# A two-layer hybrid diffusion trunk on one core: reordered modulation and attention, quarter products and a moved copy in the recurrent mixer

## The chip, the cores and the metric

The kernel runs on one core of one Trainium2 chip. The time is device microseconds of one execution; several executions of the same program are summarised by their median. The engines are PE (TensorE, matmuls; PEld is its weight load), DVE (VectorE), ACT (ScalarE), POOL (GpSimd) and SP (SyncE, which here only issues DMAs). ACT and POOL issue DMAs as well.

## The reference

Two layers are applied to 640 tokens: 128 prompt (context) tokens and 512 latent tokens, D = 1024. Cut to what matters:

```python
def trunk_layer(x, mod, P, l, ctx_cache):
    shift1, scale1, gate1, shift2, scale2, gate2 = jnp.split(mod, 6, axis=-1)   # mod = silu(c) @ w_mod[l] + b_mod[l]
    h = rms_norm(x, P['norm_mix_pre'][l]) * (1.0 + scale1) + shift1
    o, cache = mixer(h, P, l, ctx_cache)      # z = h @ w_in; heads of A, B and C; o = concat @ w_out
    x = x + gate1 * rms_norm(o, P['norm_mix_post'][l])
    h = rms_norm(x, P['norm_ffn_pre'][l]) * (1.0 + scale2) + shift2
    gu = h @ P['w_gu'][l]
    f = (jax.nn.silu(gu[..., :FF_DIM]) * gu[..., FF_DIM:]) @ P['w_down'][l]
    return x + gate2 * rms_norm(f, P['norm_ffn_post'][l]), cache

def wkv_step(S, inp):                          # mixer C: 6 heads of 64, two directions
    r, w, k, v, a, b = inp
    sa = jnp.einsum('bhvk,bhk->bhv', S, a)
    S = S * w[:, :, None, :] + sa[..., None] * b[:, :, None, :] + v[..., None] * k[:, :, None, :]
    return S, jnp.einsum('bhvk,bhk->bhv', S, r)
```

Mixers A (4 heads, window and sink) and B (6 heads, normed q and k) are softmax attention. The prompt has its own conditioning vector.

## The kernel before, in words

One program of `trunk_kernel` (L211) runs both layers. Tokens stand in five tiles of 128, taken in the order 4, 1, 2, 0, 3 (tile 4 is the prompt). Large weights are split into a high and a low part (`split`, a cast on ACT at L364 and a subtraction on DVE at L365), and each such product is three matmuls. A layer has these stages, in order:

- **Modulation.** `mod_pieces` (L466) makes a list of pieces from `mod_bias` (L415 to L419), `mod_chunk` (L384 to L391) and `mod_rows` (L421 to L450). A chunk loads 512 KB of `w_mod` as 128 rows of four pieces of 256 numbers, and multiplies it with four matmuls into four groups of 32 columns of one PSUM bank (L391). A group (one third of a layer's modulation) has 16 chunks. Group (0, 0) runs at the start of the program through `raw_tile`, a ring of three slots, beside the loads of x, which ACT issues (L562). Groups (0, 1) and (0, 2) run inside the attention loop of layer 0, two pieces at every second step. Layer 1's groups take another way (`mod_part`, DVE) during the FFN of layer 0.
- **Norm and in-projection.** `norm_tile` (L505) squares (L509), scales (L511, L512), transposes on PE (L517) and applies the modulation (L521, L524), then splits (L528, L529). `mm_tile` (L613 to L620) makes the heads; its weights come through SP (L377).
- **Attention.** A `Unit` (L791) is one pair of query heads by query tile: scores (L812, L813), peak (L829 to L844), norm (L846), turn (transposes, L853 to L865), mix (L867 to L874). The loop at L892 runs scores of unit n, then norm and turn of unit n − LAG, then mix of unit n − LAG − LAG2, with LAG = LAG2 = 1. A scheduler sets the order of the instructions on each engine there.
- **Recurrent mixer.** Five groups g of 128 tokens. `front(g)` (L1039 to L1142) prepares decays (tanh L1051, L1063), keys and gates (L1068 to L1088), and, per direction d and half cc of the group, the products of b and k with W (L1100): six matmuls into two PSUM tiles, one per head of a pair, with two copies by ACT (L1105) and two masks by DVE (L1106) and two more masks into W (L1109). `front` ends in 24 small matmuls (L1119) whose result goes to memory as `dN` (L1122). `relay(g)` (L1144 to L1159) reads it back, inverts the 16x16 blocks with 30 small POOL instructions (L1152, L1154), makes a transposed copy `VT` with DVE (L1156) and writes both to `dV`, `dW` (L1158). `solve(g)` loads them (L1166) and multiplies (L1174, L1185, L1195); `rec`, `bonus` and `finalize` follow. PE's order is written by hand: a string `WEAVE` names the stream that gives PE's next piece, under `tc.manual_schedule(engines={PE})` (L1446).
- **Out-projection, FFN.** `mm_fm` (L537) and `mm_tm` (L547).

PE, DVE, ACT and POOL each take their instructions in order, so an instruction that waits holds what is behind it on its engine. SP's DMAs are issued in order too.

Of the kernel before, what the change touches and what calls it, by code (L numbers as in the profile page):

```python
# [13 lines left out]
AF = mybir.ActivationFunctionType  # L14
# [7 lines left out]
KD = 8  # L22
# [16 lines left out]
WEAVE = ("aqqaaqaqaqqaqqqaaqqaqaqqqaqaaqqqqqqqqqccababbbbbccccbbcddcbdbcdcbbdcbdbgdcbddgeggegegeggffggegefgfgeeeeeehfgffgjjjjjjhffjihhhhjhjhhhjjhjjhjmmijikiiiimiimmkkmmmlkkmmmmkmkklklkllkklrlnnllnnmvonmnvnnrnrnvnonoovvvoorwwpooropprwwwsspwsssswpspswswppppwuppwttwtxstwuuyttxttyuuyxtutututttuutuuuuu",  # L39
         "aqqaaqaqaqqaqqqaaqqaqaqqqaqaaqqqqqqqqqccababbbbbccccbbcddcbdbcdcbbdcbdbgdcbddgeggegegeggffggegefgfgeeeeeehfgffgjjjjjjhffjihhhhjhjhhhjjhjjhjmmijikiiiimiimmkkmmmlkkmmmmkmkklklkllkklrlnnllnnmvonmnvnnrnrnvnonoovvvoorwwpooropprwwwsspwsssswpspswswppppwuppwttwtxstwuuyttxttyuuyxtutututttuutuuuuu")  # L40
# [82 lines left out]
def places(mem):  # L123
# [39 lines left out]
    mem.lay("N", 0, ("VD", 768), ("WD", 768), ("U", 256), ("tp", 64))  # L163
    mem.lay("M", 0, *many("W", (0, 1), 1536), *many("GB", (0, 1), 768), *many("TK", (2, 3), 768), *many("E", (0, 1), 384), *many("Xi", (0, 1), 384))
# [46 lines left out]
def trunk_kernel(ctx, tc, I, O, dbg=None, depth=DEPTH):  # L211
# [254 lines left out]
    def mod_pieces(groups, ps, n, slot, dma, ac=None, ahead=2):  # L466

        pieces = []
        for l, gi in groups:
            pieces.append(lambda l=l, gi=gi: mod_bias(ps, l, gi, slot()[0:4, 0:512]))  # L470
# [5 lines left out]
            else:  # L476
                for k in range(KD):
                    for c0 in range(0, 512, n):
                        pieces.append(lambda l=l, gi=gi, k=k, c0=c0: mod_chunk(ps, l, gi, k, c0, n, slot()[:, 0:4 * n], dma))
            pieces.append(lambda l=l, gi=gi: mod_rows(l, gi, ps, slot()[:, 0:512]))  # L480
        live = deque()
        for f in pieces + [None] * ahead:
            if f is not None:
                live.append(f())
                next(live[-1])
            if f is None or len(live) > ahead:
                next(live.popleft(), None)
                yield
# [16 lines left out]
    def norm_tile(p_, xt, hg, sc, sh):  # L505
        xn, h32 = nt["xn"](), nt["h32"]()
        tk = slice(128 * p_, 128 * p_ + 128)
        ssq = small.tile([128, 1], F32, tag="nss", name="nss")
        nc.scalar.activation(out=xn, in_=xt, func=AF.Square, accum_out=ssq)  # L509
# [45 lines left out]
    for l in range(depth):  # L555
        if True:
            acc = bank(0, 1, 4, 5, 6)
            if l == 0:
                hg = open_h()
                open_nt(2)  # L560
                for t in ORDER:
                    nc.scalar.dma_start(out=xt[t], in_=I["x_sample"][0, 128 * t:128 * t + 128] if t < 4 else I["x_prompt"][0])  # L562
                run(mod_pieces([(0, 0)], psb[:, 7], 256, raw_tile, nc.sync))
# [20 lines left out]

            cs = mem.get("cs", [4, 2, 32])
# [1030 lines left out]
```

## Time and profile before

| what | before |
|---|---|
| median of 3 runs | 2181.96 us (2177.76 to 2182.04) |
| the profiled execution | 2174.8 us |
| its span | 2172.8 us |
| mean granted TensorE clock | 0.953 |
| PE busy | 1972.3 us (91%) |
| PEld busy | 1727.2 us (79%) |
| DVE busy | 1205.6 us (55%) |
| ACT busy | 829.4 us (38%) |
| POOL busy | 348.6 us (16%) |
| DMA | 192.13 MB, mean 88 GB/s |

Times in the rows are microseconds from the start of the span, unless a mean is given in ns. A busy share is an average over stages with different limits; so the stretches of the program are read one by one below. A row such as "7.29 <-DVE F L1051" says that the engine stood idle for 7.29 us and that the DVE instruction of line 1051 ended it. The granted clock is the share of full speed that the throttle gave to TensorE: 0.50 is 1.2 GHz, 1.00 is 2.4 GHz.

### The profile page before, as it was taken

To read this page: it belongs to the slowest core of one execution; us is meant where nothing else is said; L and a number is where in the kernel's file an instruction comes from. 1 tells how busy PE (TensorE), PEld (TensorE's weight loads), DVE (VectorE), ACT (ScalarE), POOL (GpSimd) and SP (SyncE) were. 2 spreads that over 40 slices of the span, in tenths; PEclk is the share of its full clock that TensorE was granted. 3 is DMA by queue.
4 is the path that set the end of the run, shared out by engine and by line. 5 is a ranking of instruction groups with operands and counts; after the bars stand their busy time and mean duration, and the time that the engine had idled before them with its cause. 6 is when DMAs were issued, how large, how long until landed. Compare 5 with 4: busy or idle time off the path is not lost. (4 is left out here: it accounts for less than half of the span.)

```text
span 2172.8 us, 39707 instructions
## 1 busy us (share of the span) xinstructions
PE 1972.3 (91%) x16220; PEld 1727.2 (79%) x16220; DVE 1205.6 (55%) x2369; ACT 829.4 (38%) x1827; POOL 348.6 (16%) x634
## 2 busy tenths in 40 slices
PE   4989998777999999999989999877789999999997
PEld 1766787666779989989977778866677898998996
DVE  1756754565877636566367784356667622232324
ACT  2545643342463222212245674433335522221221
POOL 0210003353022112111022000234421100000002
PEclk8999998888999999999999999977899999999998
DMA  8265211213336344344222002031242222222221
GB/s 275 82 192 163 73 36 30 37 31 69 103 116 181 122 141 146 118 145 121 82 96 80 9 1 69 14 50 26 52 127 83 88 78 78 78 66 81 78 69 49
DMA packets 280765, 192.13 MB, mean 88 GB/s; under 512 B 107316, under 2 KB 249614, under 8 KB 280584
## 3 DMA queue, kind: packets, MB, share of 16 engines
q1 hardware_dynamic: 259152, 139.41, 23.2%
q0 software_dynamic: 8800, 29.17, 4.4%
q10 hardware_dynamic: 12632, 21.03, 2.9%
q8 instruction: 127, 2.08, 0.4%
q14 instruction: 54, 0.44, 0.1%
HBM read 173.48 MB, written 16.08 MB: 87 GB/s over the span
## 5 line engine op out<-in xcount | busy, mean ns | idle before, releaser
L537 PE MATMUL psb<-H,B 128*128 128x320 f32 x2112 | 318.3, 311 | 3.1 <-DVE H L529 2.4
L537 PEld LDWEIGHTS psb<-H,B 128*128 128x128 f32 x2112 | 312.3, 189 | 7.7 <-DVE H L529 3.2
L537 PE MATMUL psb<-H,A 128*128 128x320 f32 x2016 | 306.0, 311 | 0.0
L537 PEld LDWEIGHTS psb<-H,A 128*128 128x128 f32 x2016 | 298.4, 189 | 2.2 <-issue 1.2
L365 DVE TENSOR_TENSOR A<-F,A 128x1024 fp32r<-128x1024 f32 (+1 forms) x78 | 93.3, 1196 | 137.9 <-ACT A L364 137.9
L365 DVE TENSOR_TENSOR B<-F,B 128x1024 fp32r<-128x1024 f32 (+1 forms) x78 | 94.1, 1208 | 131.4 <-ACT B L364 131.4
L494 POOL TENSOR_TENSOR r<-v,F 128x1 f32<-128x1 f32 (+1 forms) x50 | 41.9, 840 | 739.4 <-DVE v L492 728.5
L364 ACT CAST B<-F 128x1024 fp32r<-128x1024 f32 x80 | 83.0, 1037 | 179.9 <-PE psb L537 112.8
L364 ACT CAST A<-F 128x1024 fp32r<-128x1024 f32 (+1 forms) x78 | 80.0, 1025 | 187.1 <-PE psb L537 94.3
L537 PE MATMUL psb<-H,C 128*128 128x320 f32 x864 | 130.6, 309 | 0.0
L537 PEld LDWEIGHTS psb<-H,C 128*128 128x128 f32 x864 | 127.8, 188 | 0.2
L405 DVE SCALAR_TENSOR_TENSOR F<-F 128x512 f32<-128x512 f32 x168 | 114.7, 748 | 19.9 <-DMA F<-in_w_mod 14.4
L397 POOL DMA_DIRECT2D F<-in_w_mod x96 | 71.9, 749 | 327.1 <-DVE F L403 216.9
L1544 DVE TENSOR_TENSOR F<-F,psb 128x320 f32<-128x320 f32 x88 | 42.9, 487 | 121.9 <-PE psb L537 121.9
L547 PE MATMUL psb<-A,M 128*128 128x512 f32 x370 | 96.7, 390 | 0.0
L365 DVE TENSOR_TENSOR C<-F,C 128x1024 fp32r<-128x1024 f32 (+1 forms) x34 | 40.5, 1193 | 78.2 <-ACT C L364 78.1
L547 PEld LDWEIGHTS psb<-A,M 128*128 128x128 f32 x370 | 69.2, 188 | 15.4 <-issue 1.0
L831 DVE TENSOR_REDUCE mx<-psb 128x1 f32<-128x640 f32 (+3 forms) x100 | 64.4, 645 | 30.2 <-PE psb L813 25.8
L547 PE MATMUL psb<-B,M 128*128 128x512 f32 x310 | 77.6, 390 | 0.0
L1538 ACT ACTIVATE F<-psb 128x320 f32<-128x320 f32 x88 | 38.3, 435 | 97.1 <-PE psb L537 96.0
L364 ACT CAST C<-F 128x1024 fp32r<-128x1024 f32 (+1 forms) x34 | 34.7, 1022 | 91.8 <-PE psb L547 46.6
L547 PEld LDWEIGHTS psb<-B,M 128*128 128x128 f32 x310 | 58.0, 188 | 12.8 <-issue 0.8
(418 smaller groups left out, 3960.3 us busy)
## 6 DMA issues: line engine op xcount, KB each, us to landing
F<-in_w_gu SPq DMA_DIRECT2D x88, 512.0 KB
F<-in_w_mod POOLq DMA_DIRECT2D x96, 256.0 KB, 3.4
F<-in_w_in SPq DMA_DIRECT2D x40, 512.0 KB
F<-in_w_down SPq DMA_DIRECT2D x40, 512.0 KB
F<-in_w_mod SPq DMA_DIRECT2D x38, 512.0 KB
M<-in_w_mod SPq DMA_DIRECT2D x10, 512.0 KB
F<-in_w_out SPq DMA_DIRECT2D x40, 128.0 KB
F<-in_x_sample ACTq DMA_DIRECT2D x8, 512.0 KB
```

Of the source, the lines that this page charges most:

```text
L364: nc.scalar.copy(out=hi[:, :n], in_=rawt[:, :n])
L365: (eng or nc.vector).tensor_tensor(out=lo[:, :n], in0=rawt[:, :n], in1=hi[:, :n], op=ALU.subtract)
L397: dma.dma_start(out=rv, in_=w[:, :, c0:c0 + n])
L405: nc.vector.scalar_tensor_tensor(out=ac[s][:, cc], in0=r[:, cc], scalar=sT[:, k, s:s + 1], in1=ac[s][:, cc], op0=ALU.mult, op1=ALU.add)
L494: nc.gpsimd.tensor_tensor(out=r, in0=v, in1=mhalf.to_broadcast(shape), op=ALU.pow)
L537: nc.tensor.matmul(out=ps2[hf][:, :HALF], lhsT=w[:, k, :], rhs=a[k][:, tk], start=(k == 0 and q == 0), stop=(k == KD - 1 and q == 2))
L547: nc.tensor.matmul(out=ps5[t], lhsT=a[k][:, tk], rhs=w[:, kk, :], start=(first and kk == 0 and q == 0), stop=(last and kk == nk - 1 and q ...
L831: nc.vector.reduce_max(out=mx, in_=self.S, axis=AX.XY if self.nb == 5 else AX.X)
L1538: nc.scalar.activation(out=sgt[:, HALF * hf:HALF * hf + HALF], in_=pg[hf][:, :HALF], func=AF.Silu)
L1544: nc.vector.tensor_tensor(out=sgt[:, tk], in0=sgt[:, tk], in1=pu[hf][:, :HALF], op=ALU.mult)
```

## The change

Five edits. (1) A modulation chunk is two DMAs of 128 x 1024 contiguous numbers and four matmuls of 512 columns, instead of one DMA of 128 x 4 x 256 and, over two chunks, eight matmuls of 256 columns. At the start the ring has 18 slots of 512 KB, and nine chunks are under way at once; x is scaled before the modulation is there (`scale_tile`), and the loads of tables and caches move from ACT's queue to SP's, behind `w_mod`. (2) In layer 0's attention the ring is three pairs of slots, two chunks are issued ahead of the loop and one at every second step. (3) LAG is 2, and PE's order in the attention loops is written out. (4) In `front` the products of b and k are 64 x 64 quarters: twelve matmuls for six, ordered so that one PSUM tile gets what ACT copies and DVE masks at once. (5) `VT` is copied by POOL. The WEAVE strings are new. Lines of the changed kernel are higher by 2 to 29.

```diff
-KEYS, AHEAD, LAG, LAG2, VALS, PRE = 10,2,1,1,2,'kqf'
+KEYS, AHEAD, LAG, LAG2, VALS, PRE = 10, 2, 2, 1, 2, 'kqf'
-MODW, BES = 512, 1
+MODW, BES, XA = 512, 1, 5
...
-    def mod_chunk(ps, l, gi, k, c0, n, r, dma):
...
-        dma.dma_start(out=rv, in_=w[:, :, c0:c0 + n])
+    def mod_chunk(ps, l, gi, k, r2, dma):
+
+        rv = [r.rearrange("p (j c) -> p j c", j=2) for r in r2]
+        for h in range(2):
+            o = 2048 * gi + 1024 * h
+            dma.dma_start(out=r2[h], in_=I["w_mod"][l, 128 * k:128 * k + 128, o:o + 1024])
         yield
         for j in range(4):
-            nc.tensor.matmul(out=ps[32 * j:32 * j + 32, c0:c0 + n], lhsT=sT[:, k, :], rhs=rv[:, j], start=False, stop=(k == KD - 1 and c0 + n == 512))
+            nc.tensor.matmul(out=ps[32 * j:32 * j + 32, :], lhsT=sT[:, k, :], rhs=rv[j // 2][:, j % 2], start=False, stop=k == KD - 1)
...
+                load_x(nc.scalar, ORDER[:XA])
+
+                mp = [mem.get(f"mp{i}", [1024]) for i in range(18)]
+                mg0 = mod_pieces([(0, 0)], psb[:, 7], 512, Ring([mp[i:i + 2] for i in range(0, 18, 2)]), nc.sync, None, 9)
+                run(mg0, 9)
+                load_x(nc.sync, ORDER[XA:])
+                for t in ORDER:
+                    scale_tile(xt[t])
+                run(mg0)
...
-                    norm_tile(t, xt[t], hg, (l, "sc1", s), (l, "sh1", s))
+                    norm_tile(t, xt[t], hg, (l, "sc1", s), (l, "sh1", s), px, True)
...
+            ceng = nc.sync if l == 0 else nc.scalar
...
-                    nc.scalar.dma_start(out=head2(dst[:, 0])[:, :, y], in_=I[nm][0, l])
+                    ceng.dma_start(out=head2(dst[:, 0])[:, :, y], in_=I[nm][0, l])
...
-                mslot = Ring([mem.get(nm, [1024]) for nm in ("mv0", "mv1", "mw2")])
-                mg = mod_pieces([(0, 1), (0, 2)], psb[:, 7], 256, mslot, nc.sync)
+                close_w("raw")
+                ms = [mem.get(nm, [1024]) for nm in ("raw0", "raw1", "raw2", "mw2", "mv0", "mv1")]
+                mg = mod_pieces([(0, 1), (0, 2)], psb[:, 7], 512, Ring([ms[i:i + 2] for i in range(0, 6, 2)]), nc.sync)
+                run(mg, 2)
...
-            for n_ in range(len(units) + 4):
-                if n_ % 2 == 0:
-                    run(mg, 2)
+            with tc.manual_schedule(engines={PE}):
+                for n_ in range(len(units) + 5):
+                    if n_ % 2 == 0:
+                        run(mg, 1)
...
-                        pv2 = [v3(pf(), w=128) for e in range(2)]
+                        pb, pk = v3(pf(), w=128), v3(pf(), w=128)
                         for pr in range(3):
                             for e in range(2):
-                                nc.tensor.matmul(out=pv2[e][:, pr], lhsT=BK[HS[e], pr, cc, e:e + 2].rearrange("p a j -> p (a j)"), rhs=W[HS[e], e, pr, cc],
-                                                 start=True, stop=True)
+                                for h, pv in ((e, pb), (1 - e, pk)):
+                                    nc.tensor.matmul(out=pv[HS[h], pr], lhsT=BK[HS[e], pr, cc, int(h != e)], rhs=W[HS[e], e, pr, cc], start=True, stop=True)
+
+                        nc.scalar.copy(out=GB[:, cc, :, 0:64], in_=pb[:, :, 0:64])
+                        nc.vector.tensor_tensor(out=GB[:, cc, :, 64:128], in0=pb[:, :, 64:128],
+                                                in1=mK[d][:, 64:128].unsqueeze(1).to_broadcast([128, 3, 64]), op=ALU.mult)
                         for e in range(2):
-                            pv = pv2[e]
-
-                            nc.scalar.copy(out=GB[HS[e], cc, :, 0:64], in_=pv[HS[e], :, 0:64])
-                            nc.vector.tensor_tensor(out=GB[HS[e], cc, :, 64:128], in0=pv[HS[e], :, 64:128],
-                                                    in1=mK[d][HS[e], 64:128].unsqueeze(1).to_broadcast([64, 3, 64]), op=ALU.mult)
                             o = HS[1 - e]
-                            nc.vector.tensor_tensor(out=W[o, e, :, cc], in0=pv[o], in1=mK[d][o].unsqueeze(1).to_broadcast([64, 3, 128]), op=ALU.mult)
-                            yield
+                            nc.vector.tensor_tensor(out=W[o, e, :, cc], in0=pk[o], in1=mK[d][o].unsqueeze(1).to_broadcast([64, 3, 128]), op=ALU.mult)
+                        yield
...
-                nc.vector.tensor_copy(out=VT, in_=V.rearrange("p s t -> p t s"))
+                nc.gpsimd.tensor_copy(out=VT, in_=V.rearrange("p s t -> p t s"))
```

Three places show how the order of instructions moves. The first is SP's queue at the start of the program. Before, it is (in_w_mod are the chunks, in_w_in the weights of the in-projection):

```order
L416 DMA F<-in_b_mod 4x512
L388 DMA F<-in_w_mod 128x4x256 x17
L377 DMA F<-in_w_in 128x2x512 x8
L370 DMA F<-in_w_in 128x8x128 x4
L416 DMA M<-in_b_mod 4x512
```

and now it is:

```order
L419 DMA M<-in_b_mod 4x512
L391 DMA H<-in_w_mod 128x1024 x10
L391 DMA M<-in_w_mod 128x1024 x6
L611 DMA F<-in_table 128x256
L613 DMA F<-in_table 128x256
L616 DMA F<-in_b_q_norm 128x64
L617 DMA F<-in_b_k_norm 128x64
L618 DMA F<-in_cache_a_v 128x128
L619 DMA F<-in_cache_b_v 128x128
L622 DMA F<-in_cache_a_k 128x2x64 x2
L622 DMA M<-in_cache_b_k 128x2x64 x2
L379 DMA F<-in_w_in 128x2x512 x3
```

The ten small loads, which ACT issued, stand between the 16 halves of `w_mod` and the first weights of the in-projection. The last two of them write the zone M, which held the last slots of `w_mod`.

The second is PE in layer 0's attention, about one pair of units in its middle. Before, it is (L391 is the modulation, L859 and L864 turn, L873 mix, L784 the queries):

```order
L873 MATMUL psb<-M,F 64x128 x10
L391 MATMUL psb<-F 32x256
L859 MATMUL psb<-F,M 128x128 x4
L391 MATMUL psb<-F 32x256 x7
L812 MATMUL psb<-B,C 128x320
L813 MATMUL psb<-C 128x320
L812 MATMUL psb<-B,C 128x320
L813 MATMUL psb<-C 128x320
L784 MATMUL psb<-F 128x128 x2
L859 MATMUL psb<-F,M 128x128 x4
L864 MATMUL psb<-F,M 128x128 x2
```

and now it is (L394 the modulation, L839 and L840 scores, L811 the queries, L886 and L891 turn, L900 mix):

```order
L394 MATMUL psb<-F 32x512 x4
L839 MATMUL psb<-B 128x320
L840 MATMUL psb<-C,B 128x320
L839 MATMUL psb<-B 128x320
L840 MATMUL psb<-C,B 128x320
L811 MATMUL psb<-F 128x128 x2
L886 MATMUL psb<-F,M 128x128 x4
L900 MATMUL psb<-M,F 64x128 x10
L839 MATMUL psb<-B 128x320
L840 MATMUL psb<-C,B 128x320
```

Eight modulation matmuls of 256 columns per pair of units became four of 512, and the pieces of a unit stay together.

The third is the transposed copy of the small inverses in layer 0, second group. Before, DVE takes it between pieces of `front` (L1083 to L1085 keys, L1051 the tanh, L1195 `solve`):

```order
L1195 TENSOR_TENSOR F<-psb,N 128x384 x2
L1083 TENSOR_TENSOR A<-C,F 64x6x64
L1156 COPY N<-F 96x256
L1083 TENSOR_TENSOR A<-C,F 64x6x64
L1084 SCALAR_TENSOR_TENSOR F<-F 128x6x64
L1085 TENSOR_TENSOR F<-F 128x6x64
L1051 TENSOR_SCALAR F<-F 128x384
```

and now it stands on POOL, behind the last steps of the inverses (L1180, L1182) and ahead of POOL's part of the keys (L1111):

```order
L1180 TENSOR_TENSOR N<-F,N 96x15
L1182 TENSOR_TENSOR F<-F,N 96x15
L1184 COPY N<-F 96x256
L1175 MEMSET F 96x256
L1176 MEMSET F 96x16
L1102 TENSOR_TENSOR F<-F 128x3x128
L1111 TENSOR_TENSOR A<-F 64x6x64 x2
```

The same three rows of DVE follow each other with nothing of the relay between them.

## Rows read from the trace of the kernel before

**Rows 1.** Busy time by stretch: stretch, its length, then each engine's busy us, clock, DMA share, GB/s

```profile
0.00:45.70 45.70, 20.85 (x146) 5.32 (x146) 4.19 (x23) 7.41 (x13) 2.14 (x10) 0.88 0.89 287
45.70:51.20 5.50, 2.02 (x12) 1.43 (x8) 2.76 (x9) 3.25 (x7) 0.00 (x0) 0.50 0.77 238
...
114.80:133.50 18.70, 12.31 (x82) 9.18 (x80) 5.09 (x16) 4.30 (x13) 5.49 (x9) 0.84 0.97 285
133.50:259.00 125.50, 121.42 (x1090) 86.00 (x1086) 88.63 (x302) 77.38 (x213) 1.70 (x4) 0.97 0.39 127
...
316.00:600.00 284.00, 228.92 (x3304) 197.22 (x3304) 181.84 (x348) 114.51 (x296) 93.48 (x218) 0.87 0.26 54
...
1190.70:1203.30 12.60, 10.50 (x65) 10.26 (x64) 7.37 (x22) 5.41 (x17) 0.00 (x0) 0.86 0.15 43
1203.30:1307.80 104.50, 96.11 (x828) 76.38 (x826) 87.25 (x296) 77.63 (x216) 0.00 (x0) 1.00 0.02 7
...
1364.00:1663.00 299.00, 243.41 (x3345) 209.13 (x3344) 189.30 (x358) 121.94 (x308) 92.40 (x217) 0.86 0.26 56
```

**Rows 2.** The same view, two stretches of the start: with x beside w_mod, then w_mod alone

```profile
13.50:24.00 10.50, 2.92 (x24) 0.60 (x24) 1.82 (x10) 3.64 (x7) 1.10 (x2) 1.00 1.04 384
36.00:44.50 8.50, 3.69 (x32) 0.60 (x24) 0.00 (x0) 0.00 (x0) 0.00 (x0) 0.50 0.97 297
```

**Rows 3.** Waits of PE in the first 70 us: us in total, times, longest

```profile
PE psb L391 <- DMA F<-in_w_mod: 19.3, 14, 4.2
```

**Rows 4.** Timeline: SP's loads of w_in, PE's transposes, first in-projection product; start, duration

```profile
43.32 14.18 SPq L377 DMA_DIRECT2D F<-in_w_in  x6
...
50.35 1.12 PE L517 MATMUL psb<-F 128*128 128x128 f32 x4 [2.78 <-ACT F L521]
51.20 1.22 PE L620 MATMUL psb<-B,H 128*128 128x512 f32 x2
```

**Rows 5.** Timeline of PE: modulation ahead of and inside layer 0's attention

```profile
132.47 1.08 PE L391 MATMUL psb<-F 128*32 128x256 f32 x8 [6.39 <-DMA F<-in_w_mod]
...
159.90 0.62 PE L391 MATMUL psb<-F 128*32 128x256 f32 x2
...
161.12 1.06 PE L391 MATMUL psb<-F 128*32 128x256 f32 x14
...
184.24 1.05 PE L419 MATMUL psb<-M,F 4*32 4x512 f32 x6
```

**Rows 6.** Waits of DVE and PE in layer 0's recurrent stretch: us in total, times, longest

```profile
DVE N L1156 <- POOL F L1154: 26.2, 5, 7.0
...
PE psb L1063 <- DVE F L1051: 21.4, 7, 7.9
```

**Rows 7.** One pair of these on the timeline, DVE and PE, and the clock of the stretch around it

```profile
406.88 0.37 DVE L1156 COPY N<-F 96x256 f32<-96x256 f32 x1 [5.80 <-POOL F L1154]
...
409.82 1.45 PE L1063 MATMUL psb<-F 128*128 128x130 f32 x5 [7.29 <-DVE F L1051]
...
406.00:423.00 17.00, 10.61 (x114) 9.53 (x114) 12.69 (x25) 6.89 (x20) 8.07 (x11) 0.64 0.48 70
```

**Rows 8.** Timeline of PE: the six products of a site, and the small matmuls that end front

```profile
325.78 0.94 PE L1100 MATMUL psb<-M,F 64*128 64x128 f32 x12
...
344.25 0.91 PE L1119 MATMUL psb<-F,M 64*64 64x64 f32 x24
...
386.65 0.91 PE L1119 MATMUL psb<-F,H 64*64 64x64 f32 x24
```

**Rows 9.** Groups of instructions by line in layer 0's recurrent stretch: count, busy us, mean ns

```profile
L1106 DVE TENSOR_TENSOR H<-psb,F 64x192 f32<-64x192 f32 x16 | 5.6, 352 | 4.2 <-ACT H L1105 4.1
...
L1105 ACT COPY H<-psb 64x192 f32<-64x192 f32 x16 | 5.0, 313 | 15.2 <-PE psb L1100 10.7 <-PE psb L1017 3.7 <-PE psb L1228 0.6
...
L1088 POOL COPY F<-F 128x6 f32<-128x6 f32 x10 | 4.0, 402 | 0.6
```

**Rows 10.** Timeline: PE's first product with the second group's inverses

```profile
419.78 1.44 PE L1174 MATMUL psb<-N,H 64*64 64x64 f32 x22
```

More of the change, by code (lines that the diff above doesn't have):

```diff
@@ L469, in mod_pieces @@
         for l, gi in groups:
-            pieces.append(lambda l=l, gi=gi: mod_bias(ps, l, gi, slot()[0:4, 0:512]))
+            one = lambda: slot() if ac else slot()[0]
+            pieces.append(lambda l=l, gi=gi: mod_bias(ps, l, gi, one()[0:4, 0:512]))
             if ac:
@@ L477, in mod_pieces @@
                 for k in range(KD):
-                    for c0 in range(0, 512, n):
-                        pieces.append(lambda l=l, gi=gi, k=k, c0=c0: mod_chunk(ps, l, gi, k, c0, n, slot()[:, 0:4 * n], dma))
-            pieces.append(lambda l=l, gi=gi: mod_rows(l, gi, ps, slot()[:, 0:512]))
+                    pieces.append(lambda l=l, gi=gi, k=k: mod_chunk(ps, l, gi, k, slot(), dma))
+            pieces.append(lambda l=l, gi=gi: mod_rows(l, gi, ps, one()[:, 0:512]))
         live = deque()
@@ L487, in mod_pieces @@
                 next(live.popleft(), None)
+                yield
+            elif not ac:
                 yield
@@ L503, in open_nt, with scale_tile @@
         nt["xn"], nt["h32"] = mem.ring("xn", n, [D]), mem.ring("hn", n, [KD, 128])
[L505 to L507 removed]
+    def scale_tile(xt, xn=None):
+        junk_ = nt["xn"]() if xn is None else xn
+        xn = xt if xn is None else xn
         ssq = small.tile([128, 1], F32, tag="nss", name="nss")
[L509 removed]
+        nc.scalar.activation(out=junk_, in_=xt, func=AF.Square, accum_out=ssq)
         r = rstd_of(ssq, 1, 1.0 / D, 1e-6, [128, 1], "n")
@@ L512, in norm_tile @@
         nc.vector.tensor_scalar(out=xn[:, 512:], in0=xt[:, 512:], scalar1=r, scalar2=None, op0=ALU.mult)
+    def norm_tile(p_, xt, hg, sc, sh, px=px, scaled=False):
+        xn, h32 = xt if scaled else nt["xn"](), nt["h32"]()
+        if not scaled:
+            scale_tile(xt, xn)
+        tk = slice(128 * p_, 128 * p_ + 128)
         G, S = MOD[sc], MOD[sh]
@@ L558, in trunk_kernel, with load_x @@
             if l == 0:
+                open_nt(2)
+                def load_x(eng, ts):
+                    for t in ts:
+                        eng.dma_start(out=xt[t], in_=I["x_sample"][0, 128 * t:128 * t + 128] if t < 4 else I["x_prompt"][0])
+                load_x(nc.scalar, ORDER[:XA])
[6 more added lines that the diff above has]
+                run(mg0)
+                mem.drop(*[f"mp{i}" for i in range(18)])
                 hg = open_h()
[L560 to L563, printed above, removed]
+                px = bank(2, 3, 5, 6, 4, 1)
                 for t in ORDER:
                     s = 1 if t == 4 else 0
-                    norm_tile(t, xt[t], hg, (l, "sc1", s), (l, "sh1", s))
+                    norm_tile(t, xt[t], hg, (l, "sc1", s), (l, "sh1", s), px, True)
             else:
```

58 lines of the change are left out of this document (30 added, 28 removed).

## The prediction

> **What bounds the kernel now.** I read the page first: TensorE is busy 91% of the span, so the question is where the other 9% lies and where its clock is down. The table of busy time by stretch cuts the span into stages [rows 1]. The reader is to see four of them in which PE is not full. Up to 45.7 us PE works 20.85 us while the DMA engines are busy 0.89 of the time: the first modulation waits for its weights, 19.3 us in 14 waits [rows 3], and the first in-projection product starts at 51.20 [rows 4]. From 114.8 to 133.5 PE works 12.31 of 18.70 us at a DMA share of 0.97, and the last wait there is again for w_mod, 6.39 us [rows 5]. The attention of layer 0 is PE-bound (121.42 of 125.50 us) and 21 us longer than that of layer 1 (104.50), which has no modulation in it [rows 1]. The two recurrent stretches, 284 and 299 us, have PE busy for 228.92 and 243.41 us, at a clock of 0.87 and 0.86 [rows 1]: together 110.7 us of idle PE. The waits of the first one say whose: DVE stands 26.2 us, 5 times, at the transposed copy L1156 for POOL's inverses, and PE stands 21.4 us, 7 times, at L1063 for the DVE instruction L1051 [rows 6]. The timeline ties them: DVE is held 5.80 us ahead of the copy at 406.88, L1051 is queued behind it, and PE's matmul at 409.82 has waited 7.29 us; the clock of the 17 us there is 0.64 [rows 7]. The FFN stretches are full of PE work and not touched.
>
> **The start.** Up to the last chunk the DMAs must bring 16 chunks of 512 KB (8.39 MB), x (2.62 MB) and about 0.6 MB of tables: 11.6 MB. Before, the whole stretch ran at 287 GB/s [rows 1]; w_mod alone, in pieces of 1 KB, at 297, and with the 4 KB rows of x beside it at 384 [rows 2]. The change makes every piece 4 KB and lets nine chunks be under way, so a free slot no longer paces the loads. The unknown is the rate: 297 at one end, 384 at the other. I take 384, since those are the rows of the same width: 11.6 MB / 384 = 30.2 us, and 3.5 us for the first issue and the last landing, as the first loads show it, give 34 us instead of 45.7. By the Trainium skill (DMA: Bandwidth & Descriptors, "Where 436 GB/s comes from") HBM gives a core about 358 GB/s, which binds transfers from HBM; the row of 384 GB/s stands above that, so the trace does not agree, and by the page the end would be an estimated 2.2 us later.
>
> What follows the last chunk gets longer: two cache loads stand in SP's queue between it and w_in, since they write where the last slots were. Before, the first w_in load was issued at 43.32 and its product began at 51.20, 7.9 us later, on a full DMA system [rows 4]; I take 8.7 us from the last modulation matmul (35.0) to the first product, 43.7 instead of 51.20: −7.5. x is scaled in advance and six PSUM banks take transposes, so some 16 more of the 40 transposes (each about 0.28 us at low clock, four in 1.12 [rows 4]) run before the weights are there: −4.5. Together **−12**; ends −5 (297 GB/s: 39 + 3.5 us) and −18 (the cache loads cost nothing).
>
> **The gap ahead of attention 0.** It takes 18.70 us against 12.60 at the same place in layer 1 [rows 1], and 6.39 of it is the wait for w_mod [rows 5]. Three pairs of slots are filled ahead, which should take that wait; one bias (1.05 us [rows 5]) remains: **−5**, ends −3 and −7.
>
> **Modulation inside attention 0.** Two chunks cost PE 0.62 + 1.06 us [rows 5], here about 1.65 with the overlap of the records. Now the same numbers are four matmuls of 512 columns; the bias matmuls of that width took 1.05 for six records [rows 5], so I take 0.95 for the eight of a chunk. Sixteen such chunks: 16 × (1.65 − 0.95) = −11. Not all comes back, as DVE has 88.63 us of work there [rows 1] and LAG 2 fills and drains one step more: **−9**, ends −4 and −13. PE's order being written out in both attentions I put at 0, ends −4 and +4 for layer 1: its PE is idle 8.4 us [rows 1], and half of that either way is what an order can move.
>
> **The recurrent mixer, per layer.** With the copy on POOL, which produced the inverses and is in order, DVE loses a 5.8 us hold per group [rows 7], and PE loses the waits that hang on it, 21.4 us [rows 6], −21.4. With them goes part of the low clock: 10.61 us of PE work at 0.64 [rows 7] would take 3.8 us less at 1.00; I count −3 in all, as other stalls remain. The copy itself took DVE 0.37 us [rows 7]; POOL's small copy took 0.40 [rows 9], and it stands in the relay, five times, with SP's store behind it: 5 × 0.4 = 2, of which 1 on the path, +1.
>
> What is late next: the relay. From the last product of `front` at 386.65 [rows 8] to PE's first use of the inverses at 419.78 [rows 10] are 33.1 us, while groups follow each other in 42.4 (344.25 to 386.65 [rows 8]). PE has about 34 us of work in such a period (228.92 / 284 × 42.4). So the period can fall only to somewhere near 36 to 38 us before `solve` waits for its loads; I give back 8 us of the 21 for that.
>
> The quarters: a site (5 groups × 2 directions × 2 halves = 20 per layer) has 24 records of 64 × 64 instead of 12 of 64 × 128. The trace has no such quarter of 128 columns. Nearest rows: 0.94 us for the 12 records, 0.91 for 24 of 64 × 64 × 64 [rows 8]. If four quarters run abreast the site costs 0.94 as before, if two, twice that. I take +0.2 each, +4 per layer, since the 24 small ones keep the pace. In return each site loses one DVE mask of 352 ns and one ACT copy of 313 [rows 9]; the two remaining act on 128 partitions and cost the same each. They lie beside PE work for the most part; −2. Sum −21.4 − 3 + 1 + 8 + 4 − 2 = −13.4; **−14** with a little more of the same in layer 1's longer stretch, for two layers **−28**; ends −26 (no new wait, quarters free) and +4 (the hold only moves) per layer.
>
> **Sum.** −12 − 5 − 9 + 0 − 28 = −54. The profiled execution took 2174.8 us (span 2172.8), so such an execution comes to 2121; the median of the runs shown is 7.2 above it, and with that the forecast is **2128 us**.
>
> **Rivals.** *The hold moves to the relay.* DVE is free, PE reaches `solve` earlier and stands there for the loads of dV and dW instead; the recurrent stretches keep their length, or nearly. For it: 33.1 us of chain, now with the copy on POOL. Against it: 9 us of slack in a period of 42.4. −12 − 5 − 9 = −26: 2156.
>
> *The start gives little.* The rate stays near 297, and cache loads and transposes hold the first product: the start gives −5, all else as forecast, 2181.96 − 47: 2135. For it: DMA share 0.97 at 297 [rows 2], so the engines look full; against it, the 384 beside.
>
> *Slower: the quarters run one after the other.* In the old form the two heads' products go to two PSUM tiles; now one tile gets quarters from both halves of the rows. If those cannot run abreast, 24 records take 24 times what one takes: 0.94 / 12 = 0.08 us if the old ones ran singly, 0.16 if two abreast, so 1.9 to 3.8 us a site, +0.9 to +2.8. At the middle, +1.8 at 40 sites is +72, and the time 2200. It decides from 54 / 40 = 1.35 us a site. Against it: L1119's 24 records, also from both halves into one tile, take 0.91, no more than 12 wide ones [rows 8]. The Trainium skill states it as a rule (TensorEngine Tiling (Array Packing), "Gotcha 1: PSUM Pressure"): different row tiles cannot access the same PSUM bank at once. The row of L1119 speaks against the rule, but with half the columns, so it doesn't settle it.
>
> **How the numbers follow.** Forecast 0.58; hold moves 0.22; start 0.12; quarters serial 0.08. What a measurement of this kernel can tell from no change is about 0.2%, 4.4 us. The first three lie under it, except where the hold moves and the quarters also cost double (0.02 same, 0.02 slower); of the last, 0.05 is slower, 0.02 same and 0.01 faster. So faster 0.88, same 0.05, slower 0.07. The range: all good ends at once would be −18 − 7 − 13 − 4 − 52 = −94, or 2088, and I stop a little short of that, at 2092; upward it takes in the moved hold (2156) and its meeting with a weak start (7 more), and as much again for quarters that cost more than 0.2, to 2170.
>
> **What would show it.** Right: no wait of DVE at the copy and none of PE at the tanh's product worth 5 us; the first in-projection product near 44 us; DMA near 384 GB/s until about 34; attention 0 near 116 us; the recurrent stretches near 270 and 285, with a clock over 0.87; the 24 quarter records of a site in about 1.1 us. Wrong: PE waits of several us at the first product of `solve` (the hold moved); 24 quarter records in 1.9 us or more; w_mod still landing after 40 us. A new wait of PE in attention, where it is now bound to a written order, would spoil the −9.

## The result, and the profile after

| what | before | changed |
|---|---|---|
| median | 2181.63 us (4 runs, 2177.76 to 2182.04) | 2147.14 us (4 runs, 2139.2 to 2150.35) |
| ratio | | 0.984 (95% interval 0.9816 to 0.9865) |
| the profiled execution, its span | 2174.8, 2172.8 us | 2146.71, 2144.9 us |
| granted clock, PE busy | 0.953, 1972.3 us | 0.951, 1957.5 us |

The change is faster by 34.5 us of the median, where 54 were forecast; the time lies in the range given. The profiled execution of the kernel before lay 7 us under its median, so the two profiles differ by 27.9 us only. The table of busy time by stretch of the changed kernel (stretch, length, busy us of PE, PEld, DVE, ACT, POOL, clock, DMA share, GB/s) answers to [rows 1]:

```profile
0.00:39.50 39.50, 26.82 (x102) 6.12 (x102) 6.20 (x33) 11.41 (x20) 3.24 (x12) 0.83 0.86 313
39.50:45.00 5.50, 2.34 (x12) 1.57 (x12) 5.02 (x13) 5.49 (x13) 0.00 (x0) 0.72 1.01 348
...
109.20:120.27 11.07, 11.07 (x72) 8.81 (x70) 5.31 (x16) 4.30 (x13) 5.23 (x8) 1.00 0.98 242
120.27:248.30 128.03, 115.16 (x986) 83.15 (x983) 92.79 (x304) 79.53 (x214) 1.50 (x4) 0.95 0.46 149
...
302.90:582.50 279.60, 228.41 (x3549) 195.87 (x3548) 170.28 (x321) 106.61 (x270) 98.24 (x223) 0.88 0.27 56
...
1186.60:1291.80 105.20, 91.23 (x828) 75.42 (x826) 88.30 (x297) 77.36 (x216) 0.00 (x0) 0.96 0.03 8
...
1347.90:1634.80 286.90, 238.60 (x3602) 203.98 (x3601) 177.23 (x332) 115.45 (x287) 96.95 (x222) 0.88 0.28 59
```

The reader is to see that the start and the gap ahead of attention 0 are shorter, that attention 0 is longer (128.03 against 125.50) though PE works 6 us less in it (PE's idle time rises from 4.1 to 12.9 us), and that the recurrent stretches have shortened, with PE's clock at 0.88 in both (0.87 and 0.86 before). To compare many kernels, the table below takes the times between the first instructions of stages in each trace (first in-projection product, first scores, first tanh products of `front`, first addition of the post-norm on DVE); attention runs from the first scores to the last mix.

| kernel | to first product | in-projection and gap | attention 0 | recurrent 0 | attention 1 | recurrent 1 | span |
|---|---|---|---|---|---|---|---|
| before | 51.2 | 82.3 | 126.1 | 299.7 | 104.2 | 305.9 | 2172.8 |
| changed | 45.0 | 75.3 | 127.8 | 295.3 | 104.8 | 291.2 | 2144.9 |
| modulation alone | 45.2 | 75.7 | 139.8 | 304.1 | 104.2 | 306.0 | 2176.6 |
| LAG 2 alone | 51.8 | 81.9 | 117.3 | 303.4 | 100.4 | 305.3 | 2166.1 |
| modulation and LAG 2 | 45.9 | 75.4 | 124.8 | 305.8 | 100.1 | 304.1 | 2159.8 |
| POOL's copy alone | 52.9 | 83.5 | 125.9 | 295.4 | 105.4 | 301.3 | 2167.8 |
| quarters alone | 52.3 | 82.0 | 124.5 | 295.7 | 105.5 | 292.8 | 2158.6 |
| changed, copy on DVE | 44.6 | 75.1 | 124.2 | 300.3 | 106.5 | 299.6 | 2151.6 |
| changed, wide products | 43.4 | 76.3 | 127.9 | 303.1 | 104.7 | 301.2 | 2161.5 |
| changed, order by scheduler | 44.8 | 75.2 | 122.4 | 292.0 | 100.2 | 290.2 | 2131.0 |
| the same, LAG 1 | 43.7 | 76.5 | 139.7 | 296.6 | 105.5 | 290.7 | 2155.2 |
| changed, LAG 1 | 45.0 | 75.6 | 167.7 | 291.6 | 153.7 | 289.3 | 2229.9 |
| changed, zeros elsewhere | 58.7 | 76.2 | 124.2 | 296.2 | 106.5 | 291.3 | 2156.1 |
| order by scheduler, sum on DVE | 43.9 | 74.5 | 122.2 | 290.8 | 99.8 | 289.8 | 2124.6 |

These are single profiles. Recurrent 0 has the same instructions in the first, third, fourth and fifth kernel and takes 299.7 to 305.8 us; attention 0 has the same instructions in the changed kernel and in those with the copy on DVE, with wide products and with the zeros elsewhere, and takes 124.2 to 127.9. So a difference of 6 us in a recurrent stretch, or of 4 in attention 0, says nothing by itself; the verdicts below rest on the ratios of the timed runs.

In the recurrent mixer the hold at the tanh is nearly gone: it was 21.4 us [rows 6] and is 3.4 (last row). PE's waits in the first recurrent stretch (us in total, times, longest) now are

```profile
PE psb L1130 <- DVE A L1133: 8.4, 1, 8.4
PE psb L1130 <- ACT F L1098: 4.6, 4, 1.7
PE psb L1130 <- DVE H L1133: 4.4, 4, 1.8
PE psb L1202 <- DMA N<-dW: 4.2, 4, 1.8
PE psb L1092 <- DVE F L1080: 3.4, 5, 1.2
```

The one of 8.44 us can be followed on the timeline of POOL, ACT, DVE and PE (start, duration, and in brackets the idle time ahead and what ended it):

```profile
393.76 0.60 POOL L1184 COPY N<-F 96x256 f32<-96x256 f32 x1
396.39 0.31 POOL L1175 MEMSET F<- 96x256 f32 x1 [2.03 <-DMA dV<-F]
...
396.94 0.99 POOL L1102 TENSOR_TENSOR F<-F 128x384 f32<-128x384 f32 x1
...
397.96 0.88 ACT L1337 ACTIVATE F<-F 128x128 f32<-128x128 f32 x2 [6.67 <-POOL F L1102]
...
399.15 0.31 ACT L1132 COPY A<-psb 128x192 f32<-128x192 f32 x1
...
399.49 0.36 DVE L1133 TENSOR_TENSOR A<-psb,F 128x192 f32<-128x192 f32 x1 [5.88 <-ACT A L1132]
...
399.90 2.00 PE L1130 MATMUL psb<-A,F 64*64 64x128 f32 x24 [8.44 <-DVE A L1133]
```

POOL ends the relay's steps, takes the copy of `VT`, then stands 2.03 us for the store of V before it can clear V for the next relay; behind all that is L1102, a sum of tanh values. ACT's bonus instruction L1337 waits for the sum, ACT's copy of the products (L1132) is queued behind it, DVE's mask waits for the copy and PE for the mask. Part of the hold has moved from DVE's queue to POOL's.

### The profile page after: what moved, and what is told of

The parts are those of the page before. It is cut to its first block, busy times and chain, and to the rows that moved or that the text cites. A ratio compares the mean times of both kernels' runs of the same rounds, so it can differ in the third digit from the quotient of the medians.

```text
span 2144.9 us, 40077 instructions
## 1 busy us (share of the span) xinstructions
PE 1957.5 (91%) x16508; PEld 1713.4 (80%) x16508; DVE 1185.5 (55%) x2319; ACT 815.7 (38%) x1787; POOL 356.9 (17%) x644
## 5 line engine op out<-in xcount | busy, mean ns | idle before, releaser
L549 PE MATMUL psb<-H,A 128*128 128x320 f32 x2016 | 306.0, 311 | 0.0
L549 PEld LDWEIGHTS psb<-H,C 128*128 128x128 f32 x864 | 127.8, 188 | 0.2
L559 PEld LDWEIGHTS psb<-A,M 128*128 128x128 f32 x370 | 69.2, 188 | 15.4 <-issue 1.0
L1566 ACT ACTIVATE F<-psb 128x320 f32<-128x320 f32 x88 | 38.2, 435 | 97.2 <-PE psb L549 95.3
L645 PE MATMUL psb<-B,H 128*128 128x512 f32 x240 | 63.6, 410 | 9.0 <-DVE B L367 5.9
```

What stands on the lines that cost most here:

```text
L549: nc.tensor.matmul(out=ps2[hf][:, :HALF], lhsT=w[:, k, :], rhs=a[k][:, tk], start=(k == 0 and q == 0), stop=(k == KD - 1 and q == 2))
L559: nc.tensor.matmul(out=ps5[t], lhsT=a[k][:, tk], rhs=w[:, kk, :], start=(first and kk == 0 and q == 0), stop=(last and kk == nk - 1 and q ...
L645: nc.tensor.matmul(out=ps, lhsT=a[k0 + kk][:, tk], rhs=w[:, kk, :], start=(i == 0 and q == 0), stop=(i == n - 1 and q == 2))
L1566: nc.scalar.activation(out=sgt[:, HALF * hf:HALF * hf + HALF], in_=pg[hf][:, :HALF], func=AF.Silu)
```

## The experiments

Each kernel was timed in three rounds beside the kernel before; ratios are to that one, with their 95% intervals.

**1. The modulation edits alone.** Edits (1) and (2) of the change; `front`, the copy of `VT`, WEAVE, LAG and the scheduler's order in attention are those of before. Of the change's diff there remain the hunks of `mod_chunk`, `mod_pieces`, `scale_tile`, `norm_tile`, the start and the slots; against the changed kernel, in attention:

```diff
-KEYS, AHEAD, LAG, LAG2, VALS, PRE = 10, 2, 2, 1, 2, 'kqf'
+KEYS, AHEAD, LAG, LAG2, VALS, PRE = 10, 2, 1, 1, 2, 'kqf'
...
-            with tc.manual_schedule(engines={PE}):
-                for n_ in range(len(units) + 5):
+            for n_ in range(len(units) + 4):
```

> The kernel before with the modulation edits alone: wide loads and four matmuls of 512 columns, the deep start, x scaled ahead, tables on SP's queue, the three pairs of slots; attention's order left to the scheduler with LAG 1, the recurrent mixer and its weaving as before. Theory (the modulation saves what was forecast, and attention gives it back for another reason): first product near 45 us, attention 0 about 118 us (125.5 before, 128.0 with the whole change), recurrent stretches 284 and 299, execution near 2174.8 - 13 - 8 = 2154. Rival (attention 0 is held by ACT and DVE, so cheaper modulation gives nothing there): attention 0 stays at 125 us or more, near 2161.

0.998 (0.9968 to 0.9991). The start and the gap gave their 12.6 us, but attention 0 takes 139.8 us, which neither theory explains. The timeline of PE in its middle shows why:

```profile
165.62 1.04 PE L394 MATMUL psb<-F 128*32 128x512 f32 x2
166.59 0.66 PE L886 MATMUL psb<-F,M 128*128 128x128 f32 x4
167.18 1.06 PE L394 MATMUL psb<-F 128*32 128x512 f32 x6
168.17 0.41 PE L839 MATMUL psb<-B 128*128 128x320 f32 x1
```

A chunk is eight records, two for each of four column groups. In the changed kernel they follow each other and take 1.06 us together:

```profile
154.58 1.06 PE L394 MATMUL psb<-F 128*32 128x512 f32 x8
```

Here the scheduler has put a turn (L886) between the first group and the other three. The two lone records take 0.97 us (165.62 to 166.59) and the six 0.99 (167.18 to 168.17, where the next scores begin): a chunk costs twice as much when its groups are apart.

**2. LAG 2 alone**, in the kernel before:

```diff
-KEYS, AHEAD, LAG, LAG2, VALS, PRE = 10,2,1,1,2,'kqf'
+KEYS, AHEAD, LAG, LAG2, VALS, PRE = 10,2,2,1,2,'kqf'
...
-            for n_ in range(len(units) + 4):
+            for n_ in range(len(units) + 5):
```

> The kernel before with LAG 2 alone (order left to the scheduler, modulation in matmuls of 256 columns). Theory (LAG 2 gives exponentials more time, and its worth in attention 1, about 4 us, comes to attention 0 too): attention 0 about 122, attention 1 about 100 us, execution near 2167. Rival (LAG 2 only matters where the wide modulation is): both attentions within 1.5 us of 126.1 and 104.2.

0.9942 (0.9923 to 0.996). The theory holds, and attention 0 gains more than was thought: 117.3 us. LAG 2, which the forecast had at nothing or a cost, is worth 12.6 us by itself under the scheduler's order. Part of that lies in the modulation. With LAG 1 the scheduler splits 12 of the 32 narrow chunks, as in [rows 5]; here it splits two. The sixteen records of two whole chunks take 1.07 us, as long as one wide chunk (1.06):

```profile
158.28 1.07 PE L391 MATMUL psb<-F 128*32 128x256 f32 x16
```

Counted from each modulation record to PE's next instruction, idle time left out, the modulation inside attention 0 takes PE 24.4 us in the kernel before and 18.3 here.

**3. Modulation and LAG 2** (as experiment 1, with the two lines of experiment 2):

> The kernel before with the modulation edits and LAG 2, order left to the scheduler, the recurrent mixer as before. Theory (with LAG 1 the scheduler puts other matmuls between the four column groups of a chunk, so that a chunk costs 2.0 us instead of 1.0; with LAG 2 it doesn't): attention 0 falls from 139.8 to about 122 us, attention 1 from 104.2 to about 100; execution near 2154. Rival (the 14 us are waits for loads of w_mod, which LAG does not touch): attention 0 stays over 135 us.

0.9902 (0.9882 to 0.9922). Attention 0 is 124.8 us, and the modulation inside it, counted as above, takes PE 22.0 us against 34.3 in experiment 1. So the 14 us were for the most part the split chunks; the rival falls. Yet against LAG 2 alone the wide modulation still makes attention 0 longer by 7.5 us and the gap ahead of it shorter by 6.5: there it buys nothing, and its worth is the 6 us of the start. In its trace six column groups still stand alone, against 18 in experiment 1. The windows of attention 0, first of experiment 1, then of 2, then of 3:

```profile
120.90:260.70 139.80, 133.06 (x986) 84.52 (x983) 92.48 (x304) 79.40 (x214) 1.49 (x4) 0.98 0.43 136
```

```profile
133.70:251.00 117.30, 112.71 (x1096) 83.31 (x1093) 90.30 (x303) 77.97 (x213) 1.59 (x4) 0.98 0.45 140
```

```profile
121.30:246.00 124.70, 117.08 (x985) 81.99 (x983) 91.13 (x304) 78.77 (x214) 1.60 (x4) 0.97 0.47 153
```

**4. The written order of PE undone** (LAG 2 kept): the line `with tc.manual_schedule(engines={PE}):` ahead of the attention loop is left out.

> The changed kernel with PE's order in the attention loops left to the scheduler, LAG 2 kept. Theory (the written order makes PE wait where the scheduler had other work for it): PE's waits in attention 0 fall from 12.9 us of idle time to some 5, attention 0 takes 119 to 122 us instead of 128, attention 1 about 100 instead of 105; execution near 2136. Rival (LAG 2 or the loads are at fault): attention 0 stays over 126 us.

0.9779 (0.9765 to 0.9794), a median of 2131.33 us. The theory holds: attention 0 falls to 122.4 and attention 1 to 100.2 us, and PE's idle time in attention 0 is 6.3 us instead of 12.9:

```profile
120.00:242.40 122.40, 116.14 (x985) 81.48 (x983) 91.16 (x304) 78.66 (x214) 1.59 (x4) 0.99 0.48 156
```

So the written order costs about 5 us in attention 1 and, as other kernels with it have 124.2 there, 2 to 5 us in attention 0. The two stretches make up 10.0 of the 13.9 us between the two profiles; 4.3 lie in the recurrent stretches.

**5. The same with LAG 1:**

> As the one above, with LAG 1 too, so that attention's order is wholly as before, with the new modulation in it. Theory (the written order is at fault, LAG does little): within 3 us of the kernel above. Rival (LAG 2 costs, by one more step of fill and drain): 3 us or more below it.

0.9874 (0.985 to 0.9898), 21 us over experiment 4. Neither holds: the theory allowed 3 us, and the rival had this kernel below experiment 4, not above. Attention 0 is 139.7 us, as in experiment 1, with the split chunks (34.3 us of modulation again), and attention 1 is 5.3 us longer.

**6. LAG 1 in the written order:**

> The changed kernel with LAG 1, its written order of PE kept. Theory (a written order needs the longer lag, since PE then meets unfinished exponentials): slower than the changed kernel by 5 us or more, both attentions longer. Rival (LAG 2 is what costs): attention 0 and 1 shorter by 2 us or more each.

1.0255 (1.0237 to 1.0272), slower. As the theory says, and far more: in attention 0 PE waits 39 us for the scaled exponentials.

```profile
PE psb L886 <- DVE M L878: 20.9, 11, 2.4
PE psb L886 <- DVE F L878: 18.4, 10, 2.1
```

**7. The row of zeros at another place:**

```diff
-    mem.lay("M", 1280, ("zrow", 260))
+    mem.lay("N", 1536, ("zrow", 260))
```

> The changed kernel with the row of zeros, from which POOL's ten fills of dV and dW are made, at a place in SBUF that no tile of the attention shares. Theory (ACT stands 5.2 us at 133.5 us because the fourth slot of the exponentials lies on that row, and the fills land late behind w_mod): this wait and PE's 3.1 us after it are gone, the clock near 130 to 140 us is no longer 0.70, attention 0 about 4 us shorter, execution near 2142. Rival (ACT waits for its own instructions or for the store of v): the wait stays, within 1 us.

0.9871 (0.9847 to 0.9895), no gain over the changed kernel's 0.984. In the changed kernel ACT stands at the fourth exponential, and PE behind it (timeline of the changed kernel):

```profile
133.53 0.79 ACT L871 ACTIVATE M<-psb,nb 128x640 f32<-128x640 f32 x1 [5.18 <-issue]
134.47 0.63 PE L839 MATMUL psb<-B 128*128 128x320 f32 x1 [3.11 <-ACT M L871]
```

The waits of ACT in experiment 4 name what it waits for there, one of the fills:

```profile
ACT M L871 <- DMA dW<-M: 4.3, 1, 4.3
```

In this experiment the wait is gone and attention 0 takes 124.2 us, so the theory of the wait holds, though not its time. But the fills, free of their old place, are issued at 1.46 us, beside w_mod, and the first product comes at 58.7 instead of 45.0. (Attention 0 of 124.2 us is also seen in experiment 10, where the wait was 3.1 us, so its price lies within the spread.) The first fill on POOL's timeline:

```profile
1.46 0.81 POOL L316 DMA_DIRECT2D dV<-N  x1 [0.25 <-POOL F L260]
```

**8. POOL's copy alone**, in the kernel before:

```diff
-                nc.vector.tensor_copy(out=VT, in_=V.rearrange("p s t -> p t s"))
+                nc.gpsimd.tensor_copy(out=VT, in_=V.rearrange("p s t -> p t s"))
```

> The kernel before with one edit: VT is copied by POOL. Theory (the hold of DVE goes, and most of it comes back as a wait behind POOL's relay): DVE's 26 us of waits at the copy are gone, PE's waits at L1063 fall from 21 to under 10 us per layer, the recurrent stretches shorten by 3 to 8 us each. Rival 1 (the hold simply goes): 12 us or more each, execution under 2152. Rival 2 (nothing but a move): within 2 us each.

0.9944 (0.9927 to 0.996), 12 us for both layers. PE's waits at the tanh product in recurrent 0 fall from 21.4 [rows 6] to

```profile
PE psb L1063 <- DVE F L1051: 4.9, 6, 1.4
```

and the stretch gains 4.3 us. The theory holds, and more than half of the 16.5 us comes back as other waits: over the five groups of layer 0, to the last L1119, PE's idle time falls by 7.4 us (45.6 to 38.2), over those of layer 1 by 5.3 (47.3, of the row of before in experiment 9, to 42.0). Windows of the kernel before in layer 0, then of this one in both layers:

```profile
315.60:514.20 198.60, 152.97 (x2086) 132.74 (x2086) 120.72 (x246) 81.93 (x227) 79.63 (x178) 0.83 0.22 37
```

```profile
318.40:515.60 197.20, 158.99 (x2083) 137.66 (x2084) 118.57 (x242) 81.98 (x227) 81.70 (x182) 0.80 0.22 37
1363.00:1564.50 201.50, 159.49 (x2085) 138.21 (x2085) 119.23 (x243) 83.85 (x229) 82.14 (x182) 0.80 0.22 36
```

PE's busy time is longer, at a lower clock; but the kernels of experiments 1 to 3, with the instructions of before in this stretch, have 156.4 to 157.4 us in layer 0, so an effect on the clock isn't shown.

**9. Quarters alone**, in the kernel before (the change's lines in `front`, with the two `yield`s of before):

> The kernel before with one edit: the products of b and k as quarters, with as many pieces in the weave as before. Theory (quarters run four abreast, 24 records in about 0.81 us as in the changed kernel's trace, and what they take off ACT and DVE lies beside PE): a site costs PE 0 to 0.1 us less, the execution stays within 6 us of 2174.8, rather faster. Rival (the quarters are the gain of the recurrent mixer): 4 us or more less in each recurrent stretch, under 2167.

0.9916 (0.9898 to 0.9933), 18 us. The theory falls, the rival holds. PE's waits at the tanh product are as before, and its idle time over the five groups hardly moves (45.6 and 44.6 us in layer 0, 47.3 and 48.2 in layer 1). PE's busy time falls, by 4.7 us in layer 0 and by 16 in layer 1, though it has more records; its clock is 0.85 instead of 0.83 and 0.88 instead of 0.81 (layer 1 before, then this kernel in both layers):

```profile
1363.90:1570.00 206.10, 158.84 (x2084) 137.60 (x2084) 120.80 (x247) 83.85 (x229) 79.57 (x178) 0.81 0.21 36
```

```profile
316.20:509.10 192.90, 148.26 (x2326) 128.16 (x2326) 114.05 (x226) 75.32 (x207) 80.04 (x178) 0.85 0.23 38
1362.90:1553.70 190.80, 142.59 (x2325) 122.00 (x2326) 114.41 (x227) 76.97 (x209) 79.12 (x178) 0.88 0.24 39
```

The four kernels that share the recurrent mixer of before have 153.0 to 157.4 us in layer 0 and 155.3 to 158.8 in layer 1, so both values lie outside the spread. DVE and ACT each do some 7 us less. Before, DVE's masks stood behind ACT's copies of the same products there (waits of the kernel before); with quarters that wait is gone from the list. That this is what shortens PE's work isn't shown, as PE's own idle time stays.

```profile
DVE M L1106 <- ACT M L1105: 9.6, 4, 4.0
...
DVE H L1106 <- ACT H L1105: 7.3, 7, 1.8
```

**10. The changed kernel with the copy on DVE** (the line of experiment 8 the other way):

> The changed kernel with VT copied by DVE again, all else kept. Theory (the copy's move is what shortens the recurrent stretches): DVE waits at the copy about 20 us a layer again, both recurrent stretches lengthen by 4 to 12 us, execution 2155 to 2170. Rival (the new weaving and the quarters did it): within 3 us of the changed kernel's 2146.7.

0.9907 (0.989 to 0.9924), 12 us over the changed kernel by the medians, 15 by the ratios. The theory holds; in recurrent 0 the hold is back, and the wait of 8.4 us behind POOL's queue is 3.1:

```profile
DVE N L1184 <- POOL F L1182: 30.1, 5, 8.1
...
PE psb L1092 <- DVE F L1080: 18.8, 5, 6.5
...
PE psb L1130 <- DVE A L1133: 3.1, 1, 3.1
```

**11. The changed kernel with wide products** (the lines of before in `front`, with one `yield` for both heads):

> The changed kernel with six wide products a site instead of twelve quarters, and the four copies and masks they need, in as many pieces of the weave. Theory (quarters take instructions off DVE and ACT, PE meets its operands sooner and falls less often to the low clock): both recurrent stretches together longer by 8 to 18 us, clock there lower, execution about 2160. Rival (quarters and POOL's copy repair the same waits, so one of them alone would do): within 4 us of the changed kernel.

0.9904 (0.9882 to 0.9926), 12 us over the changed kernel by the medians, 14 by the ratios, 18 in the two recurrent stretches of the profiles. The theory's times hold, and copy and quarters each have their own share. Its clock holds in layer 0 alone: over the five groups PE is busy for 157.35 and 155.13 us, against 150.78 at 0.83 and 151.65 at 0.82 in the changed kernel, but in layer 1 the clock without quarters is the higher one.

```profile
301.90:501.70 199.80, 157.35 (x2086) 136.56 (x2086) 116.62 (x242) 82.00 (x227) 84.75 (x182) 0.81 0.22 37
1356.90:1556.40 199.50, 155.13 (x2084) 134.03 (x2084) 116.62 (x243) 83.88 (x229) 84.64 (x182) 0.84 0.22 37
```

**12. Experiment 4 with the sum on DVE:**

```diff
-                        nc.gpsimd.tensor_tensor(out=ch(THS[:, :, tk]), in0=ch(THS[:, :, tk]), in1=tha, op=ALU.add)
+                        nc.vector.tensor_tensor(out=ch(THS[:, :, tk]), in0=ch(THS[:, :, tk]), in1=tha, op=ALU.add)
```

> The changed kernel with attention's order left to the scheduler, and the sum of the tanh values (POOL, behind the relay's last steps, copy and fill) made by DVE. Theory (PE's longest wait of the recurrent mixer, 8 us in the third group, comes through ACT from this sum, which stands behind the relay on POOL): that wait is under 3 us in both layers, each recurrent stretch 3 to 6 us shorter than with the scheduler's order alone, execution near 2123. Rival (the relay itself sets the period, so the wait turns up at the products with the inverses): within 2 us of 2131.

0.9762 (0.974 to 0.9785), a median of 2126.96 us, the fastest kernel of the study; the interval overlaps that of experiment 4, so the last step isn't told apart. The wait through POOL's sum, 8.7 us in experiment 4, shrinks to 2.6, and in its place PE waits for the relay's own loads. So the theory is right about the wait, but the recurrent stretches are only 1.2 and 0.4 us shorter, where it had 3 to 6; the rival's mechanism is what happened. Waits of PE in recurrent 0, of experiment 4 (first row) and of this one:

```profile
PE psb L1129 <- DVE A L1132: 8.7, 1, 8.7
```

```profile
PE psb L1201 <- DMA N<-dW: 7.2, 2, 6.7
...
PE psb L1129 <- DVE A L1132: 2.6, 1, 2.6
```

## Why the prediction was right, and where it was not

The sign and the range held. The likeliest case, 2128 us, did not: 2147 lies nearer to the rival of the moved hold (2156), and the range was wide enough for both. The three edits that were timed alone multiply to 0.998 × 0.9944 × 0.9916 = 0.984, the ratio of the whole change: LAG 2, the written order and the new weaving together add nothing, within the 6 us or so that the three intervals leave open; the new weaving was not run alone. The sum of −54 was too large by 20 us. In the profiles the stretches that it has terms for come to −30.0, and the terms were off both ways. Two small sums of the prediction don't come out of its numbers: at 297 GB/s the start ends 8.5 us later than taken, which leaves −3.5 and not −5, and its chances add up to 0.89 for faster and 0.04 for the same.

**The start: −12 forecast.** To the first product −6.2, and 0.6 us is lost again in the in-projection (63.6 before; 45.0 to 109.2 now, 64.2), so −5.6. The rate was right: 401 GB/s where x is loaded beside w_mod, 371 after it.

```profile
13.50:24.00 10.50, 5.77 (x12) 0.56 (x12) 1.81 (x10) 4.61 (x8) 1.11 (x2) 0.55 1.01 401
24.00:36.00 12.00, 11.25 (x56) 3.75 (x56) 1.92 (x6) 4.31 (x8) 1.65 (x3) 0.82 0.96 371
```

Both are above the 358 GB/s that the Trainium skill (DMA: Bandwidth & Descriptors, "Where 436 GB/s comes from") gives as HBM's limit for a core, one half of the 716 GB/s that two cores share. This program runs on one core, and the trace does not agree with 358 GB/s as a limit for it. What failed is the term for the transposes, −4.5. They run among the modulation's matmuls, as forecast, but PE is then nearly full (11.25 of 12.00 us), and the last sixteen modulation records run without a wait for a load, as PE's own backlog, until 37.3 us, where 35.0 was forecast:

```profile
34.58 2.74 PE L394 MATMUL psb<-M,F 128*32 128x512 f32 x16
```

In the in-projection PE's busy time fell by 0.8 us only (60.49 to 59.70, the clock 0.97 before and 0.92 now), and its idle time rose from 3.1 to 4.5; the long wait there is for the low part of a weight:

```profile
PE psb L645 <- DVE B L367: 4.5, 1, 4.5
```

Which load is behind that wait was not tried. The rival of the weak start had the size, −5, and one of its two reasons, the transposes; its rate near 297 GB/s was not seen.

**The gap: −5.** In the profile 18.70 became 11.07, −7.6, with PE full. Right in kind, larger in size.

**Attention 0: −9; attention 1: 0.** Measured +1.7 and +0.6. Two steps failed. The first is "PE's order being written out in both attentions I put at 0". PE's busy time in attention 0 fell from 121.42 to 115.16 us, but its idle time rose from 4.1 to 12.9, and experiment 4 gives 5.4 and 4.6 us back by taking the order out. The rival wait that the prediction named last, of PE bound to a written order, is what happened. The second is the price of the old chunks, "about 1.65" for two. The row was read rightly, but what it shows is the price of a chunk that the scheduler has split; kept together the two take 1.07 us (experiment 2), as a wide chunk does. Counted as in experiment 2, the modulation inside attention 0 takes PE 16.9 us in the changed kernel instead of 24.4, and LAG 2 alone brings it to 18.3 without wide loads. Experiments 2, 3 and 5 show that the matter is how LAG, order and chunk fit: two narrow chunks of which the scheduler splits one cost 0.62 + 1.06 us [rows 5] instead of 1.07, a wide chunk that it splits 0.97 + 0.99 instead of 1.06. Narrow chunks inside attention with LAG 2 beside the other edits were not run.

**The recurrent mixer: −28.** Measured −4.4 and −14.7 in the profiles; by the ratios of experiments 8 and 9, copy and quarters alone are worth 12 and 18 us. That these add up to about 28 is luck, as both parts were wrong.

The copy was put at −15 a layer (−21.4 − 3 + 1, and 8 given back for the relay); it is −6. In layer 0 of experiment 8 the waits at the tanh product fall by 16.5 us and PE's idle time by 7.4, so 9.1 come back, about what was allowed. What failed is that the wait would go whole, as 4.9 us stay, and that the clock would rise with it, −3: no rise is seen (0.83 before, 0.80 with the copy moved). In the changed kernel more comes back: against experiment 10, 15.4 us of waits at that product are gone, and PE's idle time over the five groups of layer 0 falls by 2.0 only (44.3 to 42.3). The wait turns up behind POOL's queue, and with the sum moved, at the loads of the inverses. That is the rival of the moved hold, true there for more of the term than was given back.

The quarters were put at +2 a layer and are −9. The step that failed is the pair "+0.2 each, +4 per layer" and "they lie beside PE work for the most part; −2". A site's quarters cost PE no more than the wide products (the row below), and with the instructions that DVE and ACT lose, PE's busy time falls while its idle time stays (experiment 9). Part of it is the higher clock; what raises it stays open.

**The slower rival** is refuted by experiment 9, where the quarters alone are 18 us faster, and by one row: a site's 24 quarter records take 0.81 us up to the next product, against 0.87 for the twelve wide ones of [rows 8] (325.78 to 326.65), both at a clock of 1.00. The changed kernel, then the product behind the wide ones in the kernel before:

```profile
312.64 0.89 PE L1130 MATMUL psb<-M,F 64*64 64x128 f32 x24
313.45 1.29 PE L965 MATMUL psb<-H,A 128*128 128x320 f32 x7
```

```profile
326.65 0.56 PE L936 MATMUL psb<-H,A 128*128 128x320 f32 x2
```

Each of a site's two PSUM tiles gets quarters from both halves of the rows, and twice the records take no longer than the wide ones. The rule of the Trainium skill (TensorEngine Tiling (Array Packing), "Gotcha 1: PSUM Pressure"), that different row tiles can't access one PSUM bank at the same time, would have cost 0.9 to 2.8 us a site by the prediction's estimate; no such cost is in this row.

## What to carry to other kernels

A stall that the profile names is worth what the next chain behind it leaves over, and that chain is found by walking every in-order queue on the way (here DVE, then POOL and ACT, then the relay's loads). Before a saving is taken from a row, look whether the row shows what the instructions cost or what it costs that they were split: the forecast for the wide chunks was the second. Small instructions on another engine are not free because that engine is half idle: dropping some was worth 18 us here, though PE waited no less. Matmuls that run side by side in column groups must be kept together in the order, and a written order has to be tried against the scheduler's with the same pipelining depth.

## What the runs showed of the hardware

Two things were not expected. Column groups of 32 that are issued next to each other run together, and apart they don't: eight records in 1.06 us, two alone in 0.97. And PE's busy time can move a stretch where its idle time doesn't: quarters alone took it over the five groups of layer 1 from 158.84 to 142.59 us at a clock of 0.88 instead of 0.81, while the idle time changed by 1 us (47.3 to 48.2). That is the largest such case here: layer 0 gives 4.7 us of busy time, and in experiment 11 it is 6.6 and 3.5 us, the last at no higher clock. Why the clock falls less often with quarters alone isn't settled; the kernels differ in many short waits.
